# Weight splits of the output projection: one difference stored whole, two operands split in the tail instead of in the SSD rows

## The chip, the cores and the metric

The kernel runs on one core of a Trainium2 chip. The metric is the device time of one execution in microseconds: the median of three runs is 1204.24 us (1202.1 to 1204.54). The changed kernel is timed the same way.

Engines are named as in the profile: PE is TensorE (PEld its weight load), DVE is VectorE, ACT is ScalarE, POOL is GpSimd, SP is SyncE, which here mostly issues transfers. SPq and ACTq are transfers issued by those two.

## The reference, cut to what matters

One layer of a hybrid decoder: a pooling branch beside a Mamba-2 SSD branch, merged by gates. The SSD runs in chunks of 128 positions, in 4 groups of 8 heads; 1024 prompt positions make 8 chunks, so there are 32 (group, chunk) pairs.

```
def layer(x, c, ...):
    ...
    proj = h @ w_in
    ...
    p = (p * silu(z_pool)) @ w_pool_out
    ...
    y, ssm_new = ssd(xs, dt, A, Bm, Cm, ssm_state)
    y = (y + d_skip[:, None] * xs).reshape(b, L, D_INNER)
    y = rmsnorm(y * silu(z_ssm), ssm_norm_g)
    s = y @ w_ssm_out
    gates = sigmoid(g_raw)
    m = gates[..., :D_MODEL] * p + gates[..., D_MODEL:] * s
    x = x + gate[:, None] * (m @ w_o)
```

`w_o` is 1024 x 1024 in float32. The change concerns how `w_o` is prepared for `m @ w_o`.

## The kernel before

**Numbers in two parts.** Matrix products run on rounded float32 (`fp32r`). To keep the precision, an operand is split: the high part is the rounded copy, made by ACT; the low part is the operand minus the high part, made by POOL (sometimes DVE). A product is then three matmuls: high by high, high by low, low by high.

**Strassen form.** `m @ w_o` is done as seven products of 512 x 512 blocks. With the quarters of `w_o` named by row (upper, lower) and column (left, right), the kernel needs, besides quarters and sums that it makes elsewhere, five split operands, each 512 x 512 in high and low part:

- B11: the upper left quarter itself
- T3: lower right minus upper right
- T1: upper right minus upper left
- T2: T3 plus upper left
- T4: T2 minus lower left

**Stages.** First the input projection (PE, lines L412 and others). Then, from about 753 us to 1035 us, the *rows*: one row per (group, chunk) pair, 32 in all, numbered 0 to 31 here. In a row, PE does the SSD work of a chunk and a share of the products with `w_pool_out` and `w_ssm_out` (L227). Then the *tail*: the last eight units of `w_ssm_out`, which complete `m`, and the seven products with `w_o`, to the end.

**One chunk** (`chunk`, L1501 to L1567). SP loads `dec`, `bc`, `xb` and the gate `sz`. ACT makes `cE` (L1513); POOL masks `dec` (L1237); ACT takes eight exponentials of `dec` (L1241). PE transposes `xb` and B and multiplies B by C (L1520 to L1523). ACT copies B (`bt`, L1525) and C (`ps`, L1532; called psC in this text), DVE makes `xw` (L1529) and `xd` (L1536), ACT rounds it to `xh` (L1533) and POOL takes the low part `xl` (L1534). DVE multiplies `dec` and `cE` (L1542, L1544). PE then makes the state's update from `xh`, `bt` and `xl` (L1549 to L1551), and the inner products from `dec` and `xd` (L1253) and from `cE` and the old state `hst` (L1256). POOL scales the old state (L1557), DVE adds the update (L1559), and `finish` (L1473 to L1484) gates the result on DVE, ACT and POOL.

**What sets the order.** In the rows the instructions of PE and SP are kept in the order of the program text (`in_line`, `ORDER`). ACT, DVE and POOL are put in order by the language's scheduler, which simulates a timeline when the program is built. Each engine runs its list strictly in order: an instruction that waits holds up all behind it.

**The splits of w_o** (`wo_splits`, L1782 to L1833) are a generator that goes one step further per row from row 8 on. For each k of 0 to 3 it loads 128 rows of the upper half of `w_o` and 128 of the lower half (`row`, L1798, 512 KB each), makes the four sums on DVE (L1808, L1809, L1815, L1819) and splits the five operands. One split is a `part`: a tile `ph` of 512 KB from a ring of `PH = 3` buffers, an ACT copy into its high half (L1787), a POOL subtract into its low half (L1788), and, one step later, a store by SP into one of five arrays `wo_d` in DRAM (L1793). There are 20 parts. A part's ACT copy must wait until the store of the part three before it has left its buffer.

**In the tail,** SP loads the split B11 and T3 back into two `Y` tiles (`yb11`, `yt3`; L1927, four transfers of 1 MB), whose buffers held an operand of the rows before. Each of the first four tail units ends with `parts(m)`: ACT and POOL split the left half of a row block of `m` (`a11h`, `a11l`) and a difference (`s3h`, `s3l`; all in `cut`, L1941 and L1942). The tiles `s1h` and `s2h` are written by units 4 to 7. PE's first product that uses `yb11` and `a11l` is at L2051 to L2053, between the tail's units; `yt3` is used later.

Of the kernel before, what the change touches and what calls it, by code (L numbers as in the profile page):

```python
# [8 lines left out]
F32 = mybir.dt.float32  # L9
F32R = mybir.dt.float32r  # L10
AF = mybir.ActivationFunctionType
ALU = mybir.AluOpType
# [8 lines left out]
P = 128  # L21
# [4 lines left out]
NS = 64  # L26
# [20 lines left out]
def tile_pool_ssd_step(  # L47
# [5 lines left out]
    nc = tc.nc  # L53
    uid = [0]

    def nm(s):
        uid[0] += 1
        return f"{s}_{uid[0]}"
# [21 lines left out]
    hp = open_("hp", 8)  # L80
# [29 lines left out]
    store_ = nc.scalar.dma_start  # L110
    mm = nc.tensor.matmul
    act = nc.scalar.activation
    V = nc.vector
# [129 lines left out]
    def dram(name, shape, dt=F32):  # L243
        return dr.tile(list(shape), dt, tag=name, name=name)
# [1014 lines left out]
    def spt(shape, tag, bufs, dt=F32):  # L1259
        return sp.tile(list(shape), dt, tag=tag, name=nm(tag), bufs=bufs)  # L1260

    class Samples:
# [231 lines left out]
    szs = []  # L1494
# [225 lines left out]
    for shape, tag, bufs in (((P, 8, 64), "xd", 2), ((P, 2, P), "bt", 2), ((P, 2, 512), "ph", PH), ((P, 4, NS), "szs", 1), ((P, 512), "t2", 1),  # L1720
                             ((P, 512), "hst", 2), ((P, 512), "xw", 1), ((P, 512), "xh", 2), ((P, 512), "xl", 2)):
        ckt(shape, tag, bufs)

# [17 lines left out]
    def S_unit(g, m, done):  # L1741
        def run(w):
            rh = [yh[g][:, q] for q in range(4)]
            rl = [yl[g][:, q] for q in range(4)]
            yield from gemm_(w, rh, rl, 4, done(m))
        return (ready(ws_d[g][m]), run)
# [29 lines left out]
            yield from run(ws.pop(i))  # L1776
    pc_ = pieces()

    wo_d = [dram(f"wo{k}", [P, 2, 4, 512]) for k in range(5)]
    oB11, oT3, oT2, oT1, oT4 = range(5)  # L1780

    def wo_splits():  # L1782
        outs = []

        def part(o, k, t):
            both = ck.tile([P, 2, 512], F32R, tag="ph", name=nm("ph"), bufs=PH)
            act(both[:, 0], t, AF.Copy)  # L1787
            nc.gpsimd.tensor_tensor(both[:, 1], t, both[:, 0].bitcast(F32), ALU.subtract)  # L1788
            outs.append((wo_d[o][:, :, k], both.bitcast(F32)))

        def out():
            while outs:
                load(*outs.pop(0))  # L1793
        left_, right_ = slice(0, 512), slice(512, 1024)

        def row(o):
            t = R()
            load(t[:, :D], w_o[0, o:o + P, :])  # L1798
            return t
        up, dn = row(0), None  # L1800
        yield
        for k in range(4):
            out()
            if k:
                part(oT3, k - 1, dn[:, right_])
            old, dn = dn, row(512 + k * P)
            yield
            V.tensor_tensor(dn[:, right_], dn[:, right_], up[:, right_], ALU.subtract)  # L1808
# [6 lines left out]
            V.tensor_tensor(t2, dn[:, right_], up[:, left_], ALU.add)  # L1815
            out()
            part(oT1, k, up[:, right_])
            yield
            V.tensor_tensor(dn[:, left_], t2, dn[:, left_], ALU.subtract)  # L1819
            out()  # L1820
            part(oB11, k, up[:, left_])
            yield
            out()
            part(oT2, k, t2)
# [12 lines left out]
    FRONT = 4  # L1837
# [54 lines left out]
    mp = ctx.enter_context(tc.tile_pool(name="mp", bufs=1, side="right", reuse_waits="tile"))  # L1892
# [4 lines left out]
    def part4(name):  # L1897
        return mp.tile([P, 4, 512], F32R, tag=name, name=name, bufs=1)
# [20 lines left out]
    in_line(order)  # L1919

    lo_, up_ = slice(0, 512), slice(512, 1024)
    a11h, a11l, s3h, s3l, s1h, s2h = [part4(n) for n in ("a11h", "a11l", "s3h", "s3l", "s1h", "s2h")]
    s3 = hs.tile([P, T], F32, tag="sq", name="s3", bufs=1)

    def b_load(o, y):
        for t, c in ((0, lo_), (1, up_)):
            load(y[:, :, c].bitcast(F32), wo_d[o][:, t])  # L1927
        return y
# [11 lines left out]
    def cut(src_, hi, lo, eng=nc.gpsimd):  # L1940
        act(hi, src_.bitcast(F32), AF.Copy)  # L1941
        eng.tensor_tensor(lo, src_.bitcast(F32), hi.bitcast(F32), ALU.subtract)  # L1942
    yb11 = b_load(oB11, Y4(hp))
    yt3 = b_load(oT3, Y4(hp))

    def parts(m):
        a, k = acc[m], m % 4
        if m < 4:
            cut(a[:, lo_], a11h[:, k], a11l[:, k])
            c = s3[:, k % 2 * 512:k % 2 * 512 + 512]  # L1950
            V.tensor_tensor(c, a[:, lo_], a[:, up_], ALU.subtract)
            cut(c, s3h[:, k], s3l[:, k])
        else:
            b = acc[k]
            V.tensor_tensor(b[:, up_], b[:, up_], a[:, up_], ALU.add)
            V.tensor_tensor(b[:, lo_], b[:, up_], b[:, lo_], ALU.subtract)
            act(s2h[:, k], b[:, lo_], AF.Copy)
            act(s1h[:, k], b[:, up_], AF.Copy)

    gates = {}  # L1960

# [41 lines left out]
    run_units([tail_unit(m) for m in range(8)])  # L2003

    def w2k():
        t = w_tile(F32).rearrange("p s k c -> p s (k c)")
        return [t[:, 0], t[:, 1]]
# [122 lines left out]
    for half in range(2):  # L2130
        c = slice(half * 512, half * 512 + 512)
# [168 lines left out]
```

## Time and profile before

| what | value |
|---|---|
| median of three runs | 1204.24 us |
| lowest, highest | 1202.1, 1204.54 us |
| the profiled execution | 1202.95 us |
| its span, first to last instruction | 1201.2 us |
| mean granted clock of PE | 0.997 |
| PE busy | 1187.3 us, 99% of the span |
| DVE, ACT, POOL busy | 76%, 55%, 67% of the span |
| splits of w_o: ACT copy, POOL subtract, median of one | 626 ns, 1299 ns |
| their count in the rows | 20 and 20 |

A line of a timeline has the start and the duration in us, then engine, line of the program, operation, out <- in by the program's names, the size, and in brackets how long the engine stood idle before it and what ended that. A line of the waits has the waiting engine, its tile and line, the releaser, and the total in us, the count and the longest. A row by source line has a count and the least, median and largest duration in ns, then the first and last start in us.

### The profile page before, as it was taken

To read this page: it belongs to the slowest core of one execution; us is meant where nothing else is said; L and a number is where in the kernel's file an instruction comes from. 1 tells how busy PE (TensorE), PEld (TensorE's weight loads), DVE (VectorE), ACT (ScalarE), POOL (GpSimd) and SP (SyncE) were. 2 spreads that over 40 slices of the span, in tenths; PEclk is the share of its full clock that TensorE was granted. 3 is DMA by queue.
4 is the path that set the end of the run, shared out by engine and by line. 5 is a ranking of instruction groups with operands and counts; after the bars stand their busy time and mean duration, and the time that the engine had idled before them with its cause. 6 is when DMAs were issued, how large, how long until landed. Compare 5 with 4: busy or idle time off the path is not lost.

```text
span 1201.2 us, 25096 instructions
## 1 busy us (share of the span) xinstructions
PE 1187.3 (99%) x9270; PEld 1125.3 (94%) x9270; DVE 918.5 (76%) x1570; ACT 661.9 (55%) x1514; POOL 807.5 (67%) x681
## 2 busy tenths in 40 slices
PE   9999999999999999999999999999999999999997
PEld 8989999999999999999999999999999988999885
DVE  6994689876979578887575564797888887679976
ACT  6864366565655656454434334576787756412435
POOL 1037869876988788764777776476998879523652
PEclk9999999999999999999999999999999999999998
DMA  9736355465556455454577767988688897595894
GB/s 367 293 133 219 132 172 181 151 230 147 177 175 194 161 159 179 136 170 147 201 235 238 245 222 253 326 304 278 214 289 292 269 299 256 205 338 157 239 215 150
DMA packets 156082, 262.69 MB, mean 219 GB/s; under 512 B 31280, under 2 KB 79160, under 8 KB 155960
## 3 DMA queue, kind: packets, MB, share of 16 engines
q1 hardware_dynamic: 87208, 171.25, 42.8%
q10 hardware_dynamic: 64592, 81.91, 19.8%
q0 software_dynamic: 4160, 7.94, 3.2%
q8 instruction: 73, 1.20, 0.4%
q14 instruction: 49, 0.40, 0.1%
HBM read 173.31 MB, written 87.73 MB: 217 GB/s over the span
## 4 chain that ended last, share of the span: by engine, by line
PE 85%; POOL 5%; issue 3%; DMA 2%; DVE 2%; ACT 2%; SPq 0%; POOLq 0%; DVEq 0%; ACTq 0%
PE mm L412 24%; PE ps L412 24%; PE mm L227 16%; PE pc L412 5%; PE ps L1253 2%; PE ps L1256 2%; PE ps L963 1%; PE ps L822 1%; PE mm L822 1%; PE pc L731 1%; PE ps L1520 1%; PE pc L1342 1%; DMA xb<-xbc 1%; PE pc L741 1%; PE ps L575 1%
## 5 line engine op out<-in xcount | busy, mean ns | idle before, releaser
L227 PE MATMUL mm<-Y,w 128*128 128x352 f32 (+1 forms) x1440 | 254.9, 331 | 0.0
L227 PEld LDWEIGHTS mm<-Y,w 128*128 128x128 f32 x1440 | 235.5, 188 | 6.0 <-issue 4.8
L154 POOL TENSOR_TENSOR w<-rawA,w 128x512 fp32r<-128x512 f32 x120 | 183.0, 1529 | 78.6 <-ACT w L151 72.8
L154 POOL TENSOR_TENSOR w<-raw,w 128x512 fp32r<-128x512 f32 x90 | 157.3, 1755 | 62.3 <-ACT w L151 61.9
L412 PE MATMUL mm<-Y,w 128*128 128x272 f32 x1200 | 168.7, 289 | 0.0
L412 PE MATMUL ps<-Y,w 128*128 128x272 f32 x1200 | 167.8, 289 | 0.0
L412 PEld LDWEIGHTS mm<-Y,w 128*128 128x128 f32 x1200 | 156.8, 188 | 2.6 <-issue 1.0
L412 PEld LDWEIGHTS ps<-Y,w 128*128 128x128 f32 x1200 | 157.1, 188 | 0.8 <-issue 0.6
L1097 DVE SCALAR_TENSOR_TENSOR GA<-GA,cvT,GA 128x1112 f32<-128x1112 f32 x72 | 125.7, 1751 | 0.1
L151 ACT ACTIVATE w<-rawA 128x512 fp32r<-128x512 f32 x120 | 75.3, 628 | 90.1 <-PE ps L412 53.7
L151 ACT ACTIVATE w<-raw 128x512 fp32r<-128x512 f32 x90 | 56.1, 629 | 109.7 <-DVE raw L349 38.8
L412 PE MATMUL mm<-G,w 128*128 128x272 f32 x720 | 101.2, 289 | 0.0
L412 PE MATMUL ps<-G,w 128*128 128x272 f32 x720 | 100.6, 289 | 0.0
L412 PEld LDWEIGHTS mm<-G,w 128*128 128x128 f32 x720 | 94.0, 188 | 1.2 <-issue 0.9
L412 PEld LDWEIGHTS ps<-G,w 128*128 128x128 f32 x720 | 94.4, 188 | 0.3 <-issue 0.3
L1241 ACT ACTIVATE dec<-dec,acT 128x128 f32<-128x128 f32 x256 | 78.7, 391 | 18.2 <-POOL dec L1237 18.2
L291 POOL TENSOR_TENSOR pw<-pw 128x512 fp32r<-128x512 f32 x40 | 66.1, 1654 | 10.3 <-ACT pw L290 10.3
L412 PE MATMUL pc<-Y,w 128*128 128x272 f32 x480 | 67.2, 288 | 0.0
L412 PEld LDWEIGHTS pc<-Y,w 128*128 128x128 f32 x480 | 62.6, 188 | 0.5 <-issue 0.4
L1477 POOL TENSOR_TENSOR Y<-xb,Y 128x512 fp32r<-128x512 f32 x32 | 41.4, 1294 | 25.4 <-ACT Y L1475 25.4
L1253 PE MATMUL ps<-dec,xd 128*64 128x128 f32 (+1 forms) x576 | 52.3, 273 | 2.2 <-DVE cE L1544 1.6
L1534 POOL TENSOR_TENSOR xl<-xw,xh 128x512 fp32r<-128x512 f32 x32 | 42.4, 1325 | 13.5 <-ACT xh L1533 13.5
(544 smaller groups left out, 2684.7 us busy)
## 6 DMA issues: line engine op xcount, KB each, us to landing
rawA<-in_w_in SPq DMA_DIRECT2D x62, 512.0 KB
ws<-pw ACTq DMA_DIRECT2D x32, 512.0 KB
dec<-acs_d SPq DMA_DIRECT2D x32, 512.0 KB
w<-ws SPq DMA_DIRECT2D x32, 512.0 KB
xbc<-GA ACTq DMA_DIRECT2D x24, 512.0 KB
wo<-ph SPq DMA_DIRECT2D x20, 512.0 KB
Y<-wo SPq DMA_DIRECT2D x10, 1024.0 KB
pw<-in_w_ssm_out ACTq DMA_DIRECT2D x32, 256.0 KB
```

What stands on the lines that cost most here:

```text
L151: ins = act(hi[:, :, :ncols], raw[:, :, :ncols], AF.Copy)
L154: (eng or nc.gpsimd).tensor_tensor(lo[:, :, :ncols], raw[:, :, :ncols], hi[:, :, :ncols].bitcast(F32), ALU.subtract)
L227: mm(ps[:, :n], w[k // 4][h][:, k % 4, :], r[k][:, o:o + n], start=(j == 0), stop=(j == len(terms) - 1))
L291: nc.gpsimd.tensor_tensor(raw.bitcast(F32R), raw, hi.bitcast(F32), ALU.subtract)
L412: mm(p, w[j // 8][:, k], A(k, s)[j // 4 == 1], start=(j == 0), stop=(j == 11))
L822: mm(held["pr", b, t][0][:, :n], w[t, k // 4][s][:, k % 4, :], r[k][:, o:o + n], start=(j == k == 0), stop=(j == 2 and k == KT - 1))
L1097: V.scalar_tensor_tensor(d[:, :n], rp[:, k:k + n], cvT[:, 24 * k + mc:24 * k + mc + 1], d[:, :n], ALU.mult, ALU.add)
L1241: act(dec[:, h], dec[:, h], AF.Exp, bias=acT[:, c, 8 * g + h:8 * g + h + 1], scale=-1.0)
L1253: mm(o[hh], xd[:S, 2 * q + hh, :], dec[:S, 2 * q + hh], start=True, stop=state is None)
L1256: mm(o[hh], state[:, h * 64:h * 64 + 64], cE[:, h], start=False, stop=True)
L1477: nc.gpsimd.tensor_tensor(yl[g][:, :, o:o + S], v, yhc.bitcast(F32), ALU.subtract)
L1534: nc.gpsimd.tensor_tensor(xl, xw, xh.bitcast(F32), ALU.subtract)
```

## The change

- T3 gets a tile of its own (`t3`) and is stored whole, 256 KB per k, into a new array `t3_d`. Only T1, T2 and T4 are split in the rows: 12 parts, not 20, and `PH` goes from 3 to 2.
- Both row loads of a k are issued together, and a k takes four steps of the generator, with the sums earlier in it.
- B11 and T3 are loaded whole in the tail (1 MB each) by ACT's queue, right behind the copies into `sq_h`, into the buffers of the tags `s1h` and `s2h`. `halves` then splits them into the `Y` tiles: eight ACT copies and eight POOL subtracts at the end of tail unit 0, ahead of its `parts`. The real `s1h` and `s2h` are taken from their pool in unit 4.

```diff
-    PH = 3
+    PH = 2
...
-    wo_d = [dram(f"wo{k}", [P, 2, 4, 512]) for k in range(5)]
-    oB11, oT3, oT2, oT1, oT4 = range(5)
+    wo_d = [dram(f"wo{k}", [P, 2, 4, 512]) for k in range(3)]
+    t3_d = dram("t3_d", [P, 4, 512])
+    oT2, oT1, oT4 = range(3)
...
-        up, dn = row(0), None
-        yield
         for k in range(4):
-            out()
-            if k:
-                part(oT3, k - 1, dn[:, right_])
-            old, dn = dn, row(512 + k * P)
+            up, dn = row(k * P), row(512 + k * P)
             yield
-            V.tensor_tensor(dn[:, right_], dn[:, right_], up[:, right_], ALU.subtract)
+            t3, t2 = ckt([P, 512], "t3", 1), ckt([P, 512], "t2", 1)
+            V.tensor_tensor(t3, dn[:, right_], up[:, right_], ALU.subtract)
             V.tensor_tensor(up[:, right_], up[:, right_], up[:, left_], ALU.subtract)
-            out()
-            if k:
-                part(oT4, k - 1, old[:, left_])
             yield
-            t2 = ckt([P, 512], "t2", 1)
-            V.tensor_tensor(t2, dn[:, right_], up[:, left_], ALU.add)
-            out()
+            outs.append((t3_d[:, k], t3))
             part(oT1, k, up[:, right_])
+            V.tensor_tensor(t2, t3, up[:, left_], ALU.add)
             yield
+            out()
             V.tensor_tensor(dn[:, left_], t2, dn[:, left_], ALU.subtract)
-            out()
-            part(oB11, k, up[:, left_])
-            yield
-            out()
             part(oT2, k, t2)
-            if k < 3:
-                up = row(k * P + P)
             yield
-        out()
-        part(oT3, 3, dn[:, right_])
-        yield
-        out()
-        part(oT4, 3, dn[:, left_])
-        yield
-        out()
+            out()
+            part(oT4, k, dn[:, left_])
+            yield
+            out()
...
-    yb11 = b_load(oB11, Y4(hp))
-    yt3 = b_load(oT3, Y4(hp))
+    early = [mp.tile([P, 4, 512], F32, tag=tag, name=nm(tag), bufs=1) for tag in ("s1h", "s2h")]
+    store_(early[0], w_o[0, 0:512, lo_].rearrange("(k p) c -> p k c", p=P))
+    store_(early[1], t3_d)
+    yb11, yt3 = Y4(hp), Y4(hp)
+
+    def halves(t, y, k):
+        act(y[:, k, lo_], t[:, k], AF.Copy)
+        nc.gpsimd.tensor_tensor(y[:, k, up_], t[:, k], y[:, k, lo_].bitcast(F32), ALU.subtract)
...
+            for k in range(4 if m == 0 else 0):
+                halves(early[0], yb11, k)
+            for k in range(4 if m == 0 else 0):
+                halves(early[1], yt3, k)
             parts(m)
```

PE's instructions and their order stay as they are. Over the whole program ACT's list goes from 1425 to 1422 rows, POOL's from 672 to 666, DVE's from 1509 to 1507 and SP's from 420 to 414.

**ACT around chunk 29, before.** `xh_13636` is chunk 29's, `dec_13448` holds that chunk's exponentials, and `ph` is a split tile of `w_o` (the first of T2, the second of T3 at k = 3):

```order
L1787 ACTIVATE ph_13725<-t_1968_13476 128x512
L1532 ACTIVATE ps_13517<-bc_13338 128x128
L1513 ACTIVATE cE_13584<-dec_13448 128x1024
L1525 ACTIVATE bt_13633<-ps_13630 128x128
L1532 ACTIVATE ps_13630<-bc_13450 128x128
L1533 ACTIVATE xh_13636<-xw_13635 128x512
L1787 ACTIVATE ph_13845<-R_13236 128x512
L1241 ACTIVATE dec_13448<-dec_13448,acT 128x128 x8
```

The same place in the changed kernel, where `xh_13624` and `dec_13437` are chunk 29's and `ph_13594` is T4 at k = 3, the last split of the rows:

```order
L1513 ACTIVATE cE_13573<-dec_13437 128x1024
L1788 ACTIVATE ph_13594<-R_13108 128x512
L1525 ACTIVATE bt_13621<-ps_13618 128x128
L1532 ACTIVATE ps_13618<-bc_13439 128x128
L1533 ACTIVATE xh_13624<-xw_13623 128x512
L1241 ACTIVATE dec_13437<-dec_13437,acT 128x128 x8
```

The split between `xh` and the exponentials is gone; the last split stands ahead of chunk 29's `bt`.

**DVE around chunk 16, before.** `xw_12064` is chunk 16's, `xw_12175` chunk 17's; the steps at L1808 to L1819 are the four sums of `w_o` at k = 1:

```order
L1473 TENSOR_TENSOR xb_11634<-ps_11967,sz_11882 128x512
L1529 TENSOR_TENSOR xw_12064<-ps_12054,wdT 128x512
L1536 TENSOR_TENSOR xd_12070<-ps_12054,dtT 128x512
L1541 TENSOR_TENSOR bt_12062<-ps_12059,bt_12062 128x128
L1542 TENSOR_TENSOR dec_11876<-dec_11876,ps_12059 128x1024
L1559 TENSOR_TENSOR hst_12109<-hst_12109,pc_12088 128x512
L1808 TENSOR_TENSOR R_12021<-R_12021,R_11908 128x512
L1809 TENSOR_TENSOR R_11908<-R_11908 128x512
L1815 TENSOR_TENSOR t_1763_12253<-R_12021,R_11908 128x512
L1563 SCALAR_TENSOR_TENSOR ps_12092<-xb_11745,Dv,ps_12092 128x128
L1819 TENSOR_TENSOR R_12021<-t_1763_12253,R_12021 128x512
```

The same place in the changed kernel, where `xw_12067` is chunk 16's and the sums are at L1805 to L1813:

```order
L1544 TENSOR_TENSOR cE_11890<-cE_11890,ps_11937 128x1024
L1563 SCALAR_TENSOR_TENSOR ps_11972<-xb_11640,Dv,ps_11972 128x128
L1805 TENSOR_TENSOR t_1722_12022<-R_11913,R_11911 128x512
L1563 SCALAR_TENSOR_TENSOR ps_11972<-xb_11640,Dv,ps_11972 128x128
L1806 TENSOR_TENSOR R_11911<-R_11911 128x512
L1810 TENSOR_TENSOR t_1723_12023<-t_1722_12022,R_11911 128x512
L1563 SCALAR_TENSOR_TENSOR ps_11972<-xb_11640,Dv,ps_11972 128x128
L1813 TENSOR_TENSOR R_11913<-t_1723_12023,R_11913 128x512
L1563 SCALAR_TENSOR_TENSOR ps_11972<-xb_11640,Dv,ps_11972 128x128
L1529 TENSOR_TENSOR xw_12067<-ps_12057,wdT 128x512
L1536 TENSOR_TENSOR xd_12073<-ps_12057,dtT 128x512
L1473 TENSOR_TENSOR xb_11640<-ps_11972,sz_11888 128x512
```

The four sums moved from behind chunk 16's `xw` to ahead of it, and the gating of chunk 14 (`xb`, L1473) from ahead of that `xw` to behind it.

More of the change, by code (lines that the diff above doesn't have):

```diff
@@ L1719, in tile_pool_ssd_step @@
     ck = right.__enter__()
-    for shape, tag, bufs in (((P, 8, 64), "xd", 2), ((P, 2, P), "bt", 2), ((P, 2, 512), "ph", PH), ((P, 4, NS), "szs", 1), ((P, 512), "t2", 1),
+    for shape, tag, bufs in (((P, 8, 64), "xd", 2), ((P, 2, P), "bt", 2), ((P, 2, 512), "ph", PH), ((P, 4, NS), "szs", 1), ((P, 512), "t2", 1), ((P, 512), "t3", 1),
                              ((P, 512), "hst", 2), ((P, 512), "xw", 1), ((P, 512), "xh", 2), ((P, 512), "xl", 2)):
@@ L1799, in row @@
             return t
[L1800 to L1801 removed]
         for k in range(4):
[L1803 to L1806 removed]
+            up, dn = row(k * P), row(512 + k * P)
             yield
[L1808 removed]
+            t3, t2 = ckt([P, 512], "t3", 1), ckt([P, 512], "t2", 1)
+            V.tensor_tensor(t3, dn[:, right_], up[:, right_], ALU.subtract)
             V.tensor_tensor(up[:, right_], up[:, right_], up[:, left_], ALU.subtract)
[L1810 to L1812 removed]
             yield
[L1814 to L1816 removed]
+            outs.append((t3_d[:, k], t3))
             part(oT1, k, up[:, right_])
[L1818 to L1821 removed]
+            V.tensor_tensor(t2, t3, up[:, left_], ALU.add)
             yield
             out()
+            V.tensor_tensor(dn[:, left_], t2, dn[:, left_], ALU.subtract)
             part(oT2, k, t2)
[L1825 to L1826 removed]
             yield
[L1828 to L1834 removed]
+            out()
+            part(oT4, k, dn[:, left_])
+            yield
+            out()
     wos = wo_splits()
@@ L1921, in tile_pool_ssd_step @@
     lo_, up_ = slice(0, 512), slice(512, 1024)
-    a11h, a11l, s3h, s3l, s1h, s2h = [part4(n) for n in ("a11h", "a11l", "s3h", "s3l", "s1h", "s2h")]
+    a11h, a11l, s3h, s3l = [part4(n) for n in ("a11h", "a11l", "s3h", "s3l")]
+    sums = []
     s3 = hs.tile([P, T], F32, tag="sq", name="s3", bufs=1)
@@ L1956, in parts @@
             V.tensor_tensor(b[:, lo_], b[:, up_], b[:, lo_], ALU.subtract)
-            act(s2h[:, k], b[:, lo_], AF.Copy)
-            act(s1h[:, k], b[:, up_], AF.Copy)
+            if not sums:
+                sums.extend((part4("s2h"), part4("s1h")))
+            act(sums[0][:, k], b[:, lo_], AF.Copy)
+            act(sums[1][:, k], b[:, up_], AF.Copy)
     gates = {}
@@ L2003, in tile_pool_ssd_step @@
     run_units([tail_unit(m) for m in range(8)])
+    s2h, s1h = sums
     def w2k():
```

## The prediction

> **What bounds the kernel now.** I read the page first, then TensorE's chain of waits, then the timeline around each wait. From the page: the span, the engines' busy shares, and the chain that ended last.
>
> ```profile
> span 1201.2 us, 25096 instructions
> ...
> PE 1187.3 (99%) x9270; PEld 1125.3 (94%) x9270; DVE 918.5 (76%) x1570; ACT 661.9 (55%) x1514; POOL 807.5 (67%) x681
> ...
> PE 85%; POOL 5%; issue 3%; DMA 2%; DVE 2%; ACT 2%; SPq 0%; POOLq 0%; DVEq 0%; ACTq 0%
> ```
>
> TensorE is busy for 1187.3 of 1201.2 us. The change leaves its instructions and their order as they are, so all that can move is the time TensorE waits. These are all its waits on the other engines but for some before the rows (engine, line, who released it; total, count, longest):
>
> ```profile
> PE ps L1253 <- DVE cE L1544: 1.6, 1, 1.6
> ...
> PE ps L1256 <- DVE cE L1544: 0.6, 1, 0.6
> PE ps L1253 <- DVE dec L1542: 0.5, 1, 0.5
> PE pc L1551 <- POOL xl L1534: 0.4, 1, 0.4
> ```
>
> The four lie in the rows and sum to 3.1 us; that is nearly the whole prize. From 1050 us on TensorE never waits, so whatever the change frees there is worth nothing, and what it adds there costs only if it uses up a margin. The profiled execution took 1202.95 us, 1.75 above its span and 1.29 under the median of the runs, 1204.24. The sum is made on 1202.95; the 1.29 is added at the end.
>
> **The longest wait, in the rows' third-last chunk.** TensorE's timeline (start, duration) in chunk 28, undisturbed, and in chunk 29:
>
> ```profile
> 1004.95 0.39 PE L1551 MATMUL pc<-xl,bt 128*128 128x512 f32 x1
> 1005.27 0.44 PE L1253 MATMUL ps<-dec,xd 128*64 128x128 f32 x4
> ...
> 1014.43 0.39 PE L1551 MATMUL pc<-xl,bt 128*128 128x512 f32 x1
> 1016.46 0.44 PE L1253 MATMUL ps<-dec,xd 128*64 128x128 f32 x4 [1.64 <-DVE cE L1544]
> ```
>
> From L1551 to L1253 it is 0.32 us undisturbed and 2.03 here: 1.71 lost. What led up to it on SP, POOL, ACT and DVE:
>
> ```profile
> 994.75 0.62 SPq L1793 DMA_DIRECT2D wo<-ph  x1
> ...
> 1001.78 1.05 ACT L1513 ACTIVATE cE<-dec 128x1024 f32<-128x1024 f32 x1
> ...
> 1004.64 0.63 SPq L1793 DMA_DIRECT2D wo<-ph  x1
> ...
> 1005.78 0.63 ACT L1533 ACTIVATE xh<-xw 128x512 fp32r<-128x512 f32 x1 [2.43 <-DVE xw L1529]
> ...
> 1006.93 1.10 POOL L1237 TENSOR_SCALAR_AFFINE_SELECT dec<-dec 128x1024 f32<-128x1024 f32 x1
> ...
> 1010.88 0.63 ACT L1787 ACTIVATE ph<-R 128x512 fp32r<-128x512 f32 x1 [4.46 <-DMA wo<-ph]
> 1011.42 2.44 ACT L1241 ACTIVATE dec<-dec,acT 128x128 f32<-128x128 f32 x8
> 1011.59 1.29 POOL L1788 TENSOR_TENSOR ph<-R,ph 128x512 fp32r<-128x512 f32 x1 [1.46 <-ACT ph L1787]
> 1012.83 1.04 POOL L1557 TENSOR_TENSOR hst<-hst,Elb 128x512 f32<-128x512 f32 x1
> 1013.96 1.22 DVE L1542 TENSOR_TENSOR dec<-dec,ps 128x1024 f32<-128x1024 f32 x1 [3.83 <-POOL hst L1557]
> ```
>
> ACT stands 4.46 us in front of T3's last copy, because the split buffer that it writes is still being stored by the transfer issued at 1004.64 (T1's, three parts earlier). Behind it on ACT stand the eight exponentials of chunk 29, and behind T3's subtract on POOL stands that chunk's state update; both reach DVE only at 1013.9, and TensorE waits for what DVE then does. The exponentials' own input was ready at 1006.93 + 1.10 = 1008.03, 3.4 us before they began.
>
> **What the change does to it.** T3 is no longer split in the rows, so this copy, its subtract and the wait are gone. The exponentials can start up to 3.4 us earlier, and the state update is no longer behind a split; both exceed 1.71. Term: −1.7. What could take its place: with two split buffers, T4's copy waits for the store of T1, two parts earlier. Here a buffer was free 1010.88 − 1004.64 = 6.2 us after its store's issue. In the new order T1's store of k = 3 takes the place on SP that the store at 994.75 has now, behind the small store of T3: about 995.4, so the buffer is free near 1001.6. T4's copy now comes right behind the cE step that ended at 1001.78 + 1.05, near 1002.8, and behind it ACT had 2.43 us to spare. I expect no wait; the upper bound is the same 4.46 us on ACT and 1.7 on TensorE.
>
> **The two smaller waits.** Chunk 30's 0.4 us: POOL's xl (L1534) comes right behind a split subtract; chunk 23's 0.5 + 0.6: the copy of C·B (psC, L1532) stands on ACT behind a split copy, and DVE's first step waits for it:
>
> ```profile
> 958.42 0.62 ACT L1787 ACTIVATE ph<-t 128x512 fp32r<-128x512 f32 x1
> ...
> 959.99 0.27 ACT L1532 ACTIVATE ps<-bc 128x128 f32<-128x128 f32 x1
> ...
> 960.29 0.29 DVE L1541 TENSOR_TENSOR bt<-ps,bt 128x128 fp32r<-128x128 f32 x1 [1.68 <-ACT ps L1532]
> ...
> 1020.21 1.30 POOL L1788 TENSOR_TENSOR ph<-R,ph 128x512 fp32r<-128x512 f32 x1
> ...
> 1022.87 1.31 POOL L1534 TENSOR_TENSOR xl<-xw,xh 128x512 fp32r<-128x512 f32 x1
> ```
>
> In the new order no split stands between chunk 29's and chunk 30's xl, so 1.30 us of POOL goes ahead of it: −0.4. In chunk 23 one copy of 0.62 us less is ahead of psC; of the 1.1 us I take 0.6 as gone (bounds 0 and 1.1). Sum of what goes: 1.7 + 0.4 + 0.6 = 2.7.
>
> **Work taken out of the rows and put in the tail.** Eight parts (T3 and the upper left quarter, B11; four each) leave the rows, by these rows (least/median/most ns):
>
> ```profile
> L1787 ACT ACTIVATE ph<-R x16: 614/626/636, 856.3 to 1018.2; 128x512 fp32r<-128x512 f32 x16
> ...
> L1788 POOL TENSOR_TENSOR ph<-R,ph x16: 1277/1299/1720, 858.0 to 1020.2; 128x512 fp32r<-128x512 f32 x16
> ```
>
> That is 8 × 0.626 = 5.0 us of ACT and 8 × 1.299 = 10.4 us of POOL, both off the path except where named above: nothing further gained. Eight stores of 512 KB fall away and four of 256 KB come: 3 MB less written, again hidden. SP's queue has 12 + 4 stores in place of 20. The eight parts return in the tail, ahead of the first a11h and a11l (this kernel's rows; then two stretches by windows: from:to, length, busy of PE, PEld, DVE, ACT, POOL, clock, DMA share, GB/s):
>
> ```profile
> 1057.57 2.32 SPq L1927 DMA_DIRECT2D Y<-wo  x4
> ...
> 1068.12 0.64 ACT L1941 ACTIVATE a11h<-G 128x512 fp32r<-128x512 f32 x1 [14.78 <-DVE G L1992]
> ...
> 1068.83 1.69 POOL L1942 TENSOR_TENSOR a11l<-G,a11h 128x512 fp32r<-128x512 f32 x1 [27.34 <-ACT a11h L1941]
> ...
> 1076.74 2.33 POOL L1942 TENSOR_TENSOR s3l<-s,s3h 128x512 fp32r<-128x512 f32 x1
> ...
> 1082.96 0.40 PE L2053 MATMUL pc<-Y,a11l 128*128 128x512 f32 x1
> ...
> 1035.00:1050.00 15.00, 15.00 (x98) 14.83 (x94) 6.57 (x14) 4.88 (x8) 5.34 (x8) 1.00 0.35 126
> 1058.00:1069.00 11.00, 11.00 (x68) 10.98 (x67) 6.24 (x10) 0.64 (x1) 0.17 (x1) 1.00 0.96 339
> ```
>
> The splits' target buffers are those that the four reads at 1057.57 filled before, so they come free about then: by 1058. The two loads of 1 MB are issued on ACT's queue before, where ACT is busy for 4.88 of 15 us, so two issues of about 0.6 us (as SP's stores above) cost nothing; that is a stretch at 126 GB/s; at the 213 GB/s that 339 leaves over it, 2 MB take 9.8 us, so they land by then (estimate). ACT: 8 × 0.626 from 1058 to 1063, in the 14.78 us that it waited: nothing. POOL: 8 × 1.299 ends at 1069; at the 2.33 us that s3l took, at 1058.6 + 18.6 = 1077.2. Then a11l, s3l, a11l at the durations shown (1.69 + 2.33 + 1.69) end at 1082.9 in that worst case, where TensorE takes the second a11l at 1082.96. Cost: 0, bounds 0 and 1. The reads saved on SP's queue there (4 MB become 2) free a stretch at a DMA share of 0.96 in which TensorE doesn't wait: nothing.
>
> **DVE's four steps per k, which stay four but move.** Both row loads of a k now come together, and each block of four stands about a chunk earlier: ahead of xw of chunks 11, 16, 21 and 26 (one or more steps behind it at 11 and 26) instead of 12, 17, 22 and 27. What they take, alone and in a crowd, and what margin the chunk behind them had (chunk 16: xl's end against its use):
>
> ```profile
> L1808 DVE TENSOR_TENSOR R<-R,R x4: 684/693/1850, 852.9 to 985.9; 128x512 f32<-128x512 f32 x4
> ...
> 897.14 1.73 POOL L1534 TENSOR_TENSOR xl<-xw,xh 128x512 fp32r<-128x512 f32 x1
> ...
> 897.65 1.77 DVE L1815 TENSOR_TENSOR t<-R,R 128x512 f32<-128x512 f32 x1
> ...
> 900.94 0.40 PE L1551 MATMUL pc<-xl,bt 128*128 128x512 f32 x1
> ```
>
> Margin: 900.94 − 898.87 = 2.07 us. The block costs 4 × 0.69 = 2.8 us alone, 4 × 1.77 = 7.1 if every step were as slow as the slowest here; one 0.69 step that stood ahead of xw now stands behind. So xl comes 2.1 us later (just within the margin) to 6.4 later (4.3 us of waiting). I take 0.3 us at chunks 16 and 21 together, near the lower end since the median is 0.693; that is the term for new waits.
>
> A rule bears on this. The row first: L1815 took 1.77 us, against 0.693 for the like step L1808, while POOL's xl beside it took 1.73. The Trainium skill (SBUF — State Buffer, section Who interferes with whom) says that a VectorE instruction with two SBUF inputs contends with a GpSimd instruction that reads SBUF; these two rows agree with it. By that rule alone each step of the block that meets a POOL step is slow, and the sum is that of the slower rival below; that POOL is busy for 67% of the span and the median is still 0.693 speaks for few such meetings.
>
> **The sum.** 1202.95 − 2.7 + 0.3 = 1200.55 for a profiled execution; + 1.29 = 1201.8 for the median. A difference of 0.2% (2.4 us, about what a measurement of this kernel can tell from no change) lies at 1201.8, so the forecast sits on that bound and its chance goes to both sides.
>
> **Rivals.**
> *All the rows' waits go.* Chunk 23's full 1.1 goes and nothing new comes: 1202.95 − 3.1 + 1.29 = 1201.1, and 1200.7 with the short delays in restarting. For it: every one of the four stands behind a part. Against: the new order uses other margins, of which the 2.07 us is one.
> *The wait only moves.* With two buffers instead of three, some copy of T4 or T1 waits for a store as T3 did, for up to 4.46 us of ACT with 1.7 us of it on TensorE; or DVE's block gives back as much. Only 0.4 to 1.0 then remains of the gain: about 1203.5. For it: fewer buffers with the same 6 us store. Against: the parts are 12 instead of 20.
> *Slower: DVE's block ahead of xw.* It decides from the point where the block of four delays xl by over 2.07 us, so from steps over 0.69 us on the mean. If at chunks 16 and 21 its steps take 1.25 to 1.8 us, each chunk waits 2.2 to 4.3 us (the second chunk's margin taken as the first's): 4.4 to 8.6 in all, less 2.7 that goes: +1.7 to +5.9, so about 1208 (1206 to 1210). For it: rows of 1.77 and 1.85 us. Against: the median of 0.693.
> *The tail's splits are late.* Only if they start after 1059 and all eight take 2.33 us; each us is then lost whole: 1203 to 1205.
> *Not as described:* if the target buffers in the tail come free only at TensorE's next use of them, the splits start late, which is the same rival.
>
> **How the numbers follow.** Forecast 0.46 (half of it faster by 0.2%, half within); all waits go 0.14 (faster); the wait only moves 0.24 (same); DVE's block 0.13 (slower); late splits 0.03 (mostly slower). Faster 0.23 + 0.15 = 0.38; slower 0.13 + 0.02 = 0.15; same 0.47. The range takes the three likelier cases whole, half a us for the spread of the runs under the best (1200.7), and the lower half of the slower case: 1200.0 to 1206.5. The best case bounds the gain, so the range reaches further up.
>
> **What would show it.** Right: no row for ACT's split copy waiting on a store near 1000 to 1012, TensorE's L1551 to L1253 near 0.32 us in chunk 29, POOL's eight tail subtracts done before 1078, TensorE's waits in the rows summing to under 1 us. Wrong: a wait of TensorE for xl or cE at the chunks behind DVE's block, a wait of ACT for a store, or a wait of TensorE after 1050.

## The result, and the profile after

The changed kernel takes 1199.25 us (median of nine runs, 1198.12 to 1201.6) against 1202.1 for the kernel before (nine runs, 1200.74 to 1204.54; the three runs shown ahead of the prediction were among them, and their median lay 2.1 us above the nine's; the other six have a median of 1201.7). The ratio is 0.998, 95% interval 0.9971 to 0.9989: faster by 2.4 us, between 1.3 and 3.5. The two medians themselves lie 2.85 us apart, which is inside that interval. The profiled execution took 1198.86 us.

From its page, the span, the busy shares, and then all of TensorE's waits on other engines (engine, line, releaser; total in us, count, longest):

```profile
span 1197.1 us, 25095 instructions
...
PE 1186.4 (99%) x9270; PEld 1124.3 (94%) x9270; DVE 922.6 (77%) x1570; ACT 662.2 (55%) x1514; POOL 809.3 (68%) x681
```

```profile
PE pc L731 <- POOL ones L117: 1.1, 1, 1.1
PE ps L703 <- DMA R<-in_x_sample: 0.9, 1, 0.9
PE ps L1256 <- DVE cE L1544: 0.6, 1, 0.6
PE pc L1550 <- DVE bt L1541: 0.2, 1, 0.2
PE pc L1551 <- POOL xl L1534: 0.2, 1, 0.2
```

The first two lie before the rows. In the rows 3.1 us of waiting became 1.0, all of it in chunk 23. The stalls of chunks 29 and 30 are gone. This is chunk 29, with what ACT and SP did before it:

```profile
996.89 0.57 SPq L1794 DMA_DIRECT2D wo<-ph  x1
...
1002.39 0.63 ACT L1788 ACTIVATE ph<-R 128x512 fp32r<-128x512 f32 x1 [1.70 <-DMA wo<-ph]
...
1004.53 2.45 ACT L1241 ACTIVATE dec<-dec,acT 128x128 f32<-128x128 f32 x8 [0.48 <-POOL dec L1237]
...
1013.67 0.39 PE L1551 MATMUL pc<-xl,bt 128*128 128x512 f32 x1
1013.99 0.44 PE L1253 MATMUL ps<-dec,xd 128*64 128x128 f32 x4
1014.26 0.39 PE L1256 MATMUL ps<-cE,hst 128*64 128x128 f32 x4
```

From L1551 to L1253 it is 0.32 us, as in the undisturbed chunk 28 before the change. The exponentials begin 9.1 us before L1551; before the change it was 3.0 (1011.42 and 1014.43). ACT still waits for a store, 1.70 us in front of T4's last copy (and 1.60 us in front of T4's copy of k = 1, at 911 us), but nothing that is soon needed stands behind it: ACT even stands idle for another 0.48 us ahead of the exponentials, which wait for POOL's `dec`.

In chunk 30 no split stands ahead of xl on POOL, and TensorE takes xl without a wait:

```profile
1017.98 1.28 POOL L1534 TENSOR_TENSOR xl<-xw,xh 128x512 fp32r<-128x512 f32 x1
...
1021.24 0.40 PE L1551 MATMUL pc<-xl,bt 128*128 128x512 f32 x1
```

Chunk 23 kept its stall. ACT and DVE there:

```profile
958.12 0.68 ACT L1241 ACTIVATE dec<-dec,acT 128x128 f32<-128x128 f32 x2
...
958.71 0.62 ACT L1788 ACTIVATE ph<-R 128x512 fp32r<-128x512 f32 x1
959.23 0.26 ACT L1532 ACTIVATE ps<-bc 128x128 f32<-128x128 f32 x1
959.52 0.29 DVE L1541 TENSOR_TENSOR bt<-ps,bt 128x128 fp32r<-128x128 f32 x1 [1.66 <-ACT ps L1532]
```

DVE waits 1.66 us for psC, where it waited 1.68 before. Between xh and psC stood T2's split and two steps of an older chunk before; now T4's split stands there, and two exponentials of the next chunk.

The tail's splits, POOL's list:

```profile
1055.19 5.09 POOL L1936 TENSOR_TENSOR Y<-s1h,Y 128x512 fp32r<-128x512 f32 x4 [16.80 <-ACT Y L1935]
1060.22 7.20 POOL L1936 TENSOR_TENSOR Y<-s2h,Y 128x512 fp32r<-128x512 f32 x4
1067.38 1.74 POOL L1928 TENSOR_TENSOR a11l<-G,a11h 128x512 fp32r<-128x512 f32 x1
```

The eight take 12.2 us, 1.3 each at first and up to 2.4 later. TensorE takes its first a11l at 1079.18, and has no wait in the tail.

**Where 4.1 us of span went.** The two profiled executions differ by more than the medians. Their spans can be cut at two matmuls: chunk 8's last update matmul, ahead of any w_o work, and TensorE's last matmul. Before, then after:

```profile
833.58 0.39 PE L1551 MATMUL pc<-xl,bt 128*128 128x512 f32 x1
...
1192.37 0.27 PE L2053 MATMUL ps<-Y,s3l 128*128 128x256 f32 x1
```

```profile
832.83 0.39 PE L1551 MATMUL pc<-xl,bt 128*128 128x512 f32 x1
...
1189.31 0.27 PE L2052 MATMUL ps<-Y,s3l 128*128 128x256 f32 x1
```

Up to chunk 8 the difference is 0.75 us, between the two matmuls 2.31 (358.79 to 356.48), and after the last matmul 1.0 (8.8 to 7.8). The change touches only the middle; whether the end belongs to it was tried below.

### The profile page after: what moved, and what is told of

The parts are those of the page before. It is cut to its first block, busy times and chain, and to the rows that moved or that the text cites. A ratio compares the mean times of both kernels' runs of the same rounds, so it can differ in the third digit from the quotient of the medians.

```text
span 1197.1 us, 25095 instructions
## 1 busy us (share of the span) xinstructions
PE 1186.4 (99%) x9270; PEld 1124.3 (94%) x9270; DVE 922.6 (77%) x1570; ACT 662.2 (55%) x1514; POOL 809.3 (68%) x681
## 4 chain that ended last, share of the span: by engine, by line
PE 91%; DMA 3%; DVE 2%; ACT 2%; POOL 1%; issue 1%; SPq 0%; DVEq 0%; ACTq 0%; POOLq 0%
PE mm L412 24%; PE ps L412 24%; PE mm L227 18%; PE pc L412 5%; PE ps L1253 2%; PE ps L1256 2%; PE ps L963 1%; PE ps L2052 1%; PE ps L2050 1%; PE ps L2051 1%; PE ps L822 1%; PE mm L822 1%; PE ps L1520 1%; ACT dec L1241 1%; DMA R<-in_x_sample 1%
## 5 line engine op out<-in xcount | busy, mean ns | idle before, releaser
L1253 PE MATMUL ps<-dec,xd 128*64 128x128 f32 (+1 forms) x576 | 52.1, 273 | 0.0
```

The source lines that it names most:

```text
L1253: mm(o[hh], xd[:S, 2 * q + hh, :], dec[:S, 2 * q + hh], start=True, stop=state is None)
```

## The experiments

Two theories. *One wait* (the prediction's): the gain is a few places where a split of w_o stands on ACT or POOL ahead of what the next chunk needs, above all T3's last copy, which waits for its buffer. *Less work in the rows*: the gain is the eight parts taken out, each worth about 0.3 us. *Placement alone* was a third: the same gain without the change, by moving the splits in time. Each kernel but e5, which is a single run, was timed in turns with the kernel before, on the same chip: e1 to e4 on one, e5 to e8 on a second, e9 to e12 on a third.

| kernel | ratio to before, 95% | waits of TensorE in the rows, us | chunk 8 to last matmul, us | last matmul to end, us |
|---|---|---|---|---|
| before | 1 | 3.1 | 358.8 | 8.8 |
| before again (e5) | – | 3.6 | 359.0 | 9.0 |
| changed | 0.998 (0.9971 to 0.9989) | 1.0 | 356.5 | 7.8 |
| changed again (e1) | 0.9982 (0.9973 to 0.9991) | 0.8 | 356.2 | 7.9 |
| changed, a row sooner (e2) | 0.9998 (0.9989 to 1.0006) | 2.0 | 357.3 | 7.6 |
| changed, a row later (e3) | 0.9971 (0.9959 to 0.9982) | 0 | 354.6 | 7.6 |
| the same again (e12) | 0.9974 (0.9963 to 0.9985) | 0 | 354.8 | 9.1 |
| before without T3's last split (e4) | 0.9987 (0.9978 to 0.9996) | 1.4 | 356.5 | 9.3 |
| before, one store sooner (e9) | 0.9994 (0.9986 to 1.0003) | 2.2 | 357.6 | 8.0 |
| before, only B11 to the tail (e10) | 0.9998 (0.9989 to 1.0006) | 3.0 | 358.4 | 7.9 |
| before, only T3 to the tail (e11) | 0.9989 (0.998 to 0.9997) | 1.2 | 356.4 | 7.8 |
| before, a row sooner (e6) | 0.9993 (0.9984 to 1.0002) | 1.5 | 356.9 | 7.7 |
| before, a row later (e7) | 1.0024 (1.0012 to 1.0036) | 2.1 | 357.4 | 8.4 |
| changed, the tail's subtracts twice (e8) | 1.0042 (1.0029 to 1.0054) | 0.6, and 6.3 in the tail | 363.9 | 8.4 |

The third column is from the profile's list of waits, the last two from cuts at the starts of the matmuls named above; they come from one profile of each kernel, while the ratio comes from all of its runs. In e2 and e6 the first load of `w_o` goes out some 5 us ahead of the first cut.

**e1, the changed kernel again**, unchanged.

> The changed kernel once more, for a second profile of it. In the first pair of profiles the span fell by 4.1 us: 0.96 of it came in TensorE's first 7 us, 2.1 in the rows, about 1.0 after TensorE's last matmul. Theory (one wait): only the rows' 2.1 us belongs to the change, so chunks 29 and 30 again show no stall and chunk 23 again about 1.8 us; the start and the end may come out either way by 1 us each. Rival (the tail gains too): the end, from TensorE's last matmul to the last instruction, is again about 4.1 us where the kernel before had 5.1. Median 1199 to 1200.5, 0.998 of the kernel before.

The ratio repeats, and so do chunks 29 and 30. Chunk 23 lost less (0.8 us of waits). The end was 7.9 us again (4.25 in the count of the expectation, which runs from the end of TensorE's last matmul to the start of the last instruction), which by itself favours the rival.

**e5, the kernel before again**, unchanged.

> The kernel before once more, for a second profile of it. From TensorE's last matmul to the end it had 8.6 us in its first profile and 9.0 in the run without T3's last split; the changed kernel had 7.6 and 7.7, and its two shifted forms 7.3. Theory (one wait): this is a matter of where POOL's last instructions fall against one DVE step and not of the change, so 7.3 to 9.0 can come out here. Rival (the tail gains about 1 us from the change): 8.5 to 9.1 again. In the rows, from the first stage's end to TensorE's last matmul, 1173.4 us as in the first profile, with the stalls of 1.7, 0.5 and 1.3 us again.

One run, 1202.26 us. The end was 9.0 us (8.7 in the count of the expectation, from the end of the last matmul), which again fits the rival. But e12, a form of the changed kernel, has 9.1, and e6, with the old tail, 7.7. So the change doesn't set the end. What does isn't shown. In the traces two things there vary between executions: ACT's wait for a late load of the residual (`m` from `x_prompt`), 0.70 us in the kernel before and none in its second profile, 0.91 in the changed kernel and none in e1, 1.68 in e12; and one DVE step, which took 2.17 us before and 1.06 after. From that step on DVE runs nearly without a pause to the end:

```profile
1176.63 2.17 DVE L2212 SCALAR_TENSOR_TENSOR R<-R,sso,s1h 128x512 f32<-128x512 f32 x1
```

```profile
1173.79 1.06 DVE L2211 SCALAR_TENSOR_TENSOR R<-R,sso,s1h 128x512 f32<-128x512 f32 x1
```

In the rows the second profile of before had chunk 29's 1.6 and chunk 30's 0.4 again, while its smaller waits moved: 0.8 for cE at 942 us, where the first had none, and 0.5 at 950; chunk 23 waited only 0.3 us and not 1.1.

**e4, the kernel before without T3's last split**: the last quarter of T3 is filled with the third.

```diff
             outs.append((wo_d[o][:, :, k], both.bitcast(F32)))
+            if (o, k) == (oT3, 2):
+                outs.append((wo_d[o][:, :, 3], both.bitcast(F32)))
...
         out()
-        part(oT3, 3, dn[:, right_])
         yield
```

> The kernel before without the split of T3 at k = 3, one of its 20 parts (the last quarter of T3 is filled with the third, so that quarter of the operand is wrong). Theory (one wait): this part alone makes the longest stall, so chunk 29's 1.71 us go and nearly the whole gain of the change is there: 1.5 to 2 us less than the kernel before, about 1200.4. Rival (less work in the rows): one part of the eight that the change takes out is worth an eighth of 2.4 us, 0.3 us.

Measured 0.9987, with the waits of chunks 29 and 30 gone and chunk 23's left. Chunk 29:

```profile
1014.37 0.39 PE L1551 MATMUL pc<-xl,bt 128*128 128x512 f32 x1
1014.69 0.44 PE L1253 MATMUL ps<-dec,xd 128*64 128x128 f32 x4
```

Between the two matmuls it is as short as the changed kernel, 356.5 us: in the profile, one part of twenty gives the whole of the change's effect in the rows. By the ratio it is 1.6 us (0.5 to 2.6), five times what the rival gives it, where the changed kernel gained 2.2 us on the same chip (e1); whether the difference is real isn't shown. The scheduler also put T4's last split earlier in this kernel (its subtract at 1010.90 us, 1020.21 before), which freed chunk 30.

**e9, the kernel before with one store a row sooner**, nothing taken out.

```diff
             part(oT1, k, up[:, right_])
+            if k == 3:
+                out()
             yield
```

> The kernel before with all its 20 splits; only the store of T1 at k = 3 is issued one row sooner on SP, so that its buffer is free when T3's last copy wants it. Theory (one wait): ACT no longer waits 4.5 us there, chunk 29's 1.7 us go, and chunk 30's 0.5 too, as T4's last split falls behind its xl; about 2 us less in the rows than the kernel before, 0.9985, like the run without T3's last split. Rival (less work in the rows): no work is taken out, so the same as the kernel before, 1.000. A store that holds SP up until POOL has made T1 could cost up to 1 us more.

ACT and TensorE at chunk 29:

```profile
1001.59 0.61 ACT L1787 ACTIVATE ph<-R 128x512 fp32r<-128x512 f32 x1
...
1010.54 2.43 ACT L1241 ACTIVATE dec<-dec,acT 128x128 f32<-128x128 f32 x8
...
1014.10 0.39 PE L1551 MATMUL pc<-xl,bt 128*128 128x512 f32 x1
1014.42 0.44 PE L1253 MATMUL ps<-dec,xd 128*64 128x128 f32 x4
1015.41 0.44 PE L1256 MATMUL ps<-cE,hst 128*64 128x128 f32 x4 [0.55 <-DVE cE L1544]
```

T3's last copy no longer waits, and L1253 follows L1551 in 0.32 us. But the scheduler then put the exponentials behind other work (1010.54), and 0.72 us went to cE instead (L1253 to L1256 takes 0.99, not 0.27). The rows are 1.2 us shorter, not 2; the ratio can't be told from 1. So the trace shows the wait as a cause by itself, with no work taken out; its price is about half of what was expected once the order moves with it, and the runs alone don't show it.

**e10 and e11, the two halves of the change**, each on the kernel before with 16 parts and three buffers. e10 is the diff of `early`, `halves` and `sums` for B11 alone; e11 the same for T3, stored whole from the row tile:

```diff
-            part(oB11, k, up[:, left_])
```

```diff
-            if k:
-                part(oT3, k - 1, dn[:, right_])
...
+            outs.append((t3_d[:, k], dn[:, right_]))
...
-        out()
-        part(oT3, 3, dn[:, right_])
-        yield
```

> The kernel before with half of the change: B11 loaded whole and split in the tail, T3 still split in the rows, 16 parts, three buffers. In its order T3's last copy falls in chunk 27 or 28 and T4's last behind chunk 29's exponentials, so neither stands ahead of what chunks 29 and 30 need. Theory (one wait): about 2.2 us less in the rows than before, as with the whole change; chunk 23's stall stays, since psC still stands behind a split; 0.998 to 0.9985. Rival (less work in the rows): half of the gain, 0.999.

> The kernel before with the other half: T3 stored whole from the row tile and split in the tail, B11 still split in the rows, 16 parts, three buffers. T3's last copy is gone and T4's last stands behind chunk 29's exponentials. Theory (one wait): the same 2.2 us less in the rows, chunk 23's stall stays; 0.998 to 0.9985. The two halves then don't add up, as each removes the same wait. Rival (less work in the rows): half of the gain, 0.999, and the halves add up.

By the profiles, T3 alone gives the rows what the whole change gives (356.4 us). By the runs it gives 1.3 us (0.4 to 2.4), a little less than was expected (0.998 to 0.9985) and less than the whole change's 2.4 (1.3 to 3.5); the intervals overlap, so the runs don't show whether B11's part adds anything. In the profiles B11 alone gives 0.4: chunk 29's and 30's waits are gone there too, but a new one of 1.6 us came, at chunk 22. DVE and TensorE there:

```profile
942.25 1.53 DVE L1815 TENSOR_TENSOR t<-R,R 128x512 f32<-128x512 f32 x1
...
945.62 1.33 DVE L1819 TENSOR_TENSOR R<-t,R 128x512 f32<-128x512 f32 x1
...
949.06 0.60 PE L1520 MATMUL ps<-ident,xb 128*128 128x128 f32 x4
951.22 0.30 PE L1522 MATMUL ps<-ident,bc 128*128 128x128 f32 x1 [1.56 <-DVE ps L1563]
```

TensorE waits for a PSUM tile that DVE still has to finish (L1563), behind sums of w_o that took 1.53 and 1.33 us and not 0.69: 1.48 us more, with no pause on DVE from the first of them to L1563. As many parts are out of the rows in one half as in the other, and the stretch between the two matmuls is 2 us shorter in one than in the other (medians of the runs: 1199.84 us for T3, 1200.91 for B11, though the intervals of the two ratios overlap). So the amount of work doesn't set the gain. My theory's number for e10 was wrong too: I had counted the stalls that go and not the one that comes.

**e2 and e3, the changed kernel with the splits started a row sooner or later.**

```diff
-        if i > 7:
+        if i > 6:
```

```diff
-        if i > 7:
+        if i > 8:
```

> The changed kernel with the generator of the w_o splits started one row earlier; the same work. In its order the copy psC of chunk 23 stands right behind xh, with no split and no exponentials of chunk 24 ahead of it. Theory (single places decide): chunk 23's stall of about 1.8 us goes, so 1.2 to 1.8 us less than the changed kernel, about 1198, unless the moved splits or sums stand in the way at another chunk. Rival (less work in the rows is the gain): the work is the same, so the time is the same within 0.5 us.

> The changed kernel with the generator started one row later; the sums then stand ahead of xw of chunks 12, 17, 22 and 27 as in the kernel before. psC of chunk 23 again stands right behind xh. Theory (single places decide): chunk 23's stall goes, 1.2 to 1.8 us less than the changed kernel, but T4's last copy comes about a row later, near chunk 30, where a split ahead of xl cost 0.5 us before. About 1198 to 1199. Rival (less work): the same as the changed kernel within 0.5 us.

A row later, TensorE has no wait left in the rows. psC of chunk 23 comes early, right behind xh:

```profile
955.00 0.62 ACT L1533 ACTIVATE xh<-xw 128x512 fp32r<-128x512 f32 x1
955.52 0.26 ACT L1532 ACTIVATE ps<-bc 128x128 f32<-128x128 f32 x1
955.72 2.44 ACT L1241 ACTIVATE dec<-dec,acT 128x128 f32<-128x128 f32 x8
...
960.52 0.40 PE L1551 MATMUL pc<-xl,bt 128*128 128x512 f32 x1
960.85 0.44 PE L1253 MATMUL ps<-dec,xd 128*64 128x128 f32 x4
```

A row sooner, chunk 23 is clean as well, but at 847 us TensorE (its timeline) waits for a load, and the gain is lost:

```profile
849.00 0.30 PE L1522 MATMUL ps<-ident,bc 128*128 128x128 f32 x1 [1.75 <-DMA xb<-xbc]
```

The work is the same in all three forms, and the time spans 0.9971 to 0.9998: places decide, not work.

**e12, the row later once more.**

> The changed kernel with the generator one row later once more, the fastest so far (0.9971), for a second profile. Theory (single places decide): again no stall of TensorE in the rows, 1169 us from the first stage's end to TensorE's last matmul, ratio 0.997. If 0.998 or more comes out, the first result was partly the runs' spread.

0.9974, and no wait in the rows again. Of all that was run, this form is the fastest; it beats the changed kernel (e1, on the same chip with e3: 1199.2 us against 1197.76).

**e6 and e7, the kernel before with the same shifts** (`i > 6`, `i > 8`).

> The kernel before, all 20 splits in the rows, with the generator started one row earlier. In its order chunk 29's exponentials stand ahead of the split on ACT, so a wait for the buffer holds up nothing that chunk 29 needs. Rival (placement alone): the gain of the change is one of where the splits fall, so this gives it too, 2 to 3 us less than the kernel before. Theory (one wait): the same for chunk 29's 1.7 us; but 20 parts leave more places to collide than 12, so some new stall of 0.5 to 2 us is likely and the time lands between the kernel before and the changed one. Rival (less work in the rows): the same as the kernel before within 0.5 us.

> The kernel before with the generator started one row later, the shift that made the changed kernel lose all its stalls (0.9971). Rival (placement alone): 0.997 to 0.998 here as well. Theory (one wait, and less to collide): chunk 29's stall goes, but two splits come close together on ACT ahead of chunk 31, with the ring of three buffers waiting for their stores, so a stall of 0.5 to 2 us is likely there; 0.998 to 1.000. Rival (less work in the rows): 1.000.

A row sooner takes away chunk 29's stall, but 1.5 us of waiting comes at 941 us, for DVE's cE step (TensorE's list of waits):

```profile
PE ps L1522 <- DVE cE L1544: 1.5, 1, 1.5
```

The stretch between the two matmuls is 356.9 us, so in this profile placement alone saves 1.9 of the change's 2.3 us. The runs don't bear that out: the time can't be told from before (0.9993, a gain of 0.8 us between −0.2 and 1.9). A row later is slower, 1.0024. Its runs spread from 1200.26 to 1207.73 us, and the profiled one is the fastest of them, so its profile (2.1 us of waits) doesn't show what made the others slow. That stays open. Placement alone thus wasn't shown to give the gain at either shift, but the first shift may give a part of it, and a shift can't be ruled out that gives it all.

**e8, the tail's subtracts made twice.**

```diff
         nc.gpsimd.tensor_tensor(y[:, k, up_], t[:, k], y[:, k, lo_].bitcast(F32), ALU.subtract)
+        nc.gpsimd.tensor_tensor(y[:, k, up_], t[:, k], y[:, k, lo_].bitcast(F32), ALU.subtract)
```

> The changed kernel with each of the eight POOL subtracts of the tail made twice. In its profile they ran from 1055.2 to 1067.4 us and the first a11l came at once after, needed about 13 us later. Theory (the tail hides the splits): twice takes 10 to 19 us more, so they end at 1078 to 1086; TensorE needs a11l at 1080 and 1080.7. So a loss of 0 to 7 us, likeliest 3, seen as a wait of TensorE for a11l at L2053 and nowhere else. Rival (the tail's splits already cost something): the full 10 to 19 us show in the time.

1206.06 us, 1.0042 (1.0029 to 1.0054): about 7 us above the changed kernel's 0.998. TensorE's timeline shows two waits for a11l:

```profile
1081.23 0.50 PE L2053 MATMUL pc<-Y,a11l 128*128 128x512 f32 x1 [3.06 <-POOL a11l L1928]
...
1092.28 0.50 PE L2053 MATMUL pc<-Y,a11l 128*128 128x512 f32 x1 [3.23 <-POOL a11l L1928]
```

The first wait is what was expected, 3 us. The second wasn't: the scheduler put the last two extra subtracts between POOL's a11l steps, and POOL was still late at the next a11l. So the tail hides eight subtracts, and not sixteen.

## Why the prediction was right or wrong

**The level was wrong; the size of the change was right, though two of its terms were not.** The forecast of 1201.8 was 2.55 us too high, and 1199.25 lies under the range's 1200.0. The step that failed is the last of the sum: "+ 1.29 = 1201.8 for the median". It took the three runs' median, 1204.24, as the level of the kernel. Over nine runs it is 1202.1, and over 28 beside the first experiments 1200.97 (1199.06 to 1204.3). The two highest of the nine were among the three; why they were high isn't shown. The profiled execution, at 1202.95, was itself above the middle; the 1.29 should have been about −0.85, which leads to 1199.7. The range gave the runs' spread half a us, though the three runs shown spanned 2.4; the spread is of the level, and belongs at both ends.

**The sum for the change:** −2.4 forecast, −2.4 measured by the ratio (1.3 to 3.5), −2.3 between the two matmuls of the first pair of profiles and −2.8 of the second. That the sum fits so closely is in part luck: two of its terms, −0.6 and +0.3, both came to about nothing and nearly cancel; the two that held give −2.1.

- *Chunk 29, −1.7:* right. 1.71 us lost before, 0 after, and its cause is shown from three sides (e4, e9, e11).
- *T4's wait at two buffers, none expected:* ACT did wait, 1.70 us. The store went out at 996.89 and not 995.4, and the buffer was free 5.5 us later. The 2.43 us that ACT had to spare, named as its cover, hid it: no cost to TensorE. So the prediction's own sign of being wrong, a wait of ACT for a store, came and meant nothing. Three buffers in the changed kernel weren't tried.
- *Chunk 30, −0.4:* right; POOL's xl started 1017.98, with no split ahead, and TensorE took it at 1021.24.
- *Chunk 23, −0.6:* wrong. DVE's wait for psC stayed at 1.66 us. The step counted one split copy less ahead of psC; in the new order another split, T4's of k = 2, and two exponentials stood in its place. In e3, where psC comes right behind xh, all of it goes. The size of the stall moves by itself: 1.1 and 0.3 us in two profiles of the kernel before, 1.0 and 0.8 in two of the changed one.
- *New waits, +0.3 for DVE's block at chunks 16 and 21:* none in the changed kernel, and not because the block was short. (A k takes five steps of the generator, as these chunks show, not the four named in the section on the change.) At chunk 16 the four steps took 1.67, 0.95, 0.68 and 1.80 us, 1.28 on the mean, which the slower rival prices at over 2 us of waiting. This is what xw and xl did there, before and then after:

```profile
892.33 0.68 DVE L1529 TENSOR_TENSOR xw<-ps,wdT 128x512 f32<-128x512 f32 x1
...
894.86 0.64 ACT L1533 ACTIVATE xh<-xw 128x512 fp32r<-128x512 f32 x1
```

```profile
891.87 1.80 DVE L1813 TENSOR_TENSOR R<-t,R 128x512 f32<-128x512 f32 x1
...
893.85 0.68 DVE L1529 TENSOR_TENSOR xw<-ps,wdT 128x512 f32<-128x512 f32 x1
...
894.56 0.63 ACT L1533 ACTIVATE xh<-xw 128x512 fp32r<-128x512 f32 x1 [0.72 <-DVE xw L1529]
896.67 1.28 POOL L1534 TENSOR_TENSOR xl<-xw,xh 128x512 fp32r<-128x512 f32 x1
...
900.03 0.40 PE L1551 MATMUL pc<-xl,bt 128*128 128x512 f32 x1
```

Measured from the update of the chunk ahead (L1551 at 893.37 us before and 892.47 after), xw came 2.4 us later. But before the change xh had started only 1.85 us after xw was done, and now it starts at once; xl started 0.4 us later, was itself 0.45 us shorter, and ended 2.08 us before its use, where it had been 2.07. The step took a delay of xw for a delay of xl, and left out the slack between them. A block of sums can still cost, at another place: in e10 the sums delay L1563, and TensorE waits for PSUM, not for xl.
- *The tail at 0:* right. Splits done at 1067.4 against a worst case of 1077.2; e8 shows where it would have cost.
- *The trace's span* fell by 4.1 us, 1.7 more than the sum: 0.75 before any w_o work and 1.0 after the last matmul, both of which vary from run to run by as much.

The rival *all waits go* was the nearest miss: the changed kernel keeps 1 us, and one number in the code, the row at which the splits start, would have taken it (e3). *The wait only moves* is what e10, e2 and e6 did; the changed kernel's waits in the rows sum to 1.0 us, at the edge of the prediction's sign of being right (under 1 us).

## What to carry to other kernels

On a kernel that is bound by one engine to 99%, look for the gain in the few waits of that engine, and follow each back to the instruction that holds up a list; a 4.5 us wait on ACT was worth 1.7 us for what stood behind it, and 1.70 us on ACT were worth nothing. Moving side work then shifts every list: count the stalls that may come as well as those that go, and try the same work a step sooner and later. Anchor a forecast on the spread of the runs, not on the median of three, when the effect is as large as that spread.

## What the runs showed of the hardware

The same POOL subtract took 1.30 us at the start of the tail's eight and up to 2.38 within 10 us. DVE was slower beside these subtracts too. This is the same step of the tail's gating in the kernel before, where POOL was idle (from 1041.5 to 1068.8 us), and in the changed kernel:

```profile
1064.81 1.29 DVE L1991 TENSOR_TENSOR G<-G,R 128x1088 f32<-128x1088 f32 x1
```

```profile
1061.72 2.23 DVE L1985 TENSOR_TENSOR G<-G,R 128x1088 f32<-128x1088 f32 x1
```

The first DVE step L2211 (L2212 before) took between 0.74 and 2.73 us over the profiles. In most of them it is the longer the sooner it starts behind POOL's last step there: 2.73 us where it starts 0.1 us behind (e5), 1.06 at 0.8 us (the changed kernel), 0.74 at 1.2 us (e7); e12, with 1.55 at 1.5 us, doesn't fit. With POOL mostly idle, later in the kernel before and the changed one, it took 0.74 to 0.75 each time. The Trainium skill (SBUF — State Buffer, section Who interferes with whom) names such a pair, a VectorE step with two SBUF inputs beside a GpSimd step that reads SBUF; these rows agree with it, though no run here changed the neighbour and nothing else.

One execution of one kernel moved by 1 us ahead of any difference between the kernels (chunk 8 at 833.58 and 832.60 us for the same program; on one chip 832.63 in e1 and 833.65 in e3, where all `w_o` work lies behind that point), so a single pair of spans can't tell a change of 2 us.
